# Stores on another queue, two weight splits earlier, one bank copy unpinned, and a reordered end of the down projection, in a one-core transformer layer

## The chip, the core and the metric

The kernel runs on one core of a Trainium2 chip. The metric is the device time of one execution in microseconds (us). A core has a matrix engine (TensorE, PE in the profile), a vector engine (DVE), a scalar engine (ACT), a general engine (POOL) and a queue that here only issues transfers (SP). Each engine takes its instructions in order; they wait for one another through semaphores. TensorE writes into PSUM, eight banks of 128 x 512 floats.

## The reference, cut to what matters

One layer on a sequence of 1024 tokens, width 1024, all float32:

```python
h = modulate(rms_norm(x, norm1_g), sh1, sc1)
q, k, v, g, hc, gb, gc = jnp.split(h @ w_in, 7, axis=-1)
# retention over q, k, v (4 heads, chunks of 64), a gated short convolution over hc, gb, gc
mixed = jnp.concatenate([ret_out, conv_out], axis=-1) @ w_out
x = x + gt1[:, None, :] * mixed
h = modulate(rms_norm(x, norm2_g), sh2, sc2)
u = causal_dwconv(h @ w_up, conv_ffn_w, conv_ffn_b)      # width 3, D_FF = 2816
ua, ub = jnp.split(u, 2, axis=-1)
x = x + gt2[:, None, :] * ((jax.nn.silu(ua) * ub) @ w_down)
return rms_norm(x, final_g)
```

## The kernel before

**Precision.** A float32 operand is split into a high half (a cast, mostly on ACT) and a low half (the difference, mostly on DVE), and each product is made of three matmuls: high x high, high x low, low x high. So nothing can be multiplied on PE before ACT and then DVE have worked on it.

**Tokens** are worked in 8 blocks (tb) of 128. The output projection runs in three groups, `out_mm((0, 1, 2))`, `out_mm((3, 4, 5))` and `out_mm((6, 7))`; in the last, block 7 lags a step behind block 6. Each step takes one of 8 pieces of w_out: a load into one of three raw buffers (SP, L923), the high half wo_h (ACT, L99), the low half wo_l (DVE, L100), each in one of four buffers.

**Per block**, `norm2` (L946 to L955) reloads x, multiplies the projection by the gate (DVE), adds it (L951; on DVE or POOL), stores the result as x1 (SP, L952), sums its squares (ACT, L165), makes the reciprocal root in two small POOL instructions (`rstd_of`, L159 and L160) and scales the row (DVE, L955). `norm2_T` transposes the scaled row on PE (x1T), modulates it on the way out of PSUM (ACT L989, DVE L991), and, for blocks 0 to 3, stores it as h_d (SP, L993) and splits it into h2[0]. For blocks 4 to 7 it reloads the row of block tb - 4 (hu) and forms the sums and differences that a seven-product (Strassen) scheme needs, splitting them into h2[1], h2[2] and h2[3].

**The up projection** works on 22 pairs of weight blocks (n), each in seven products over the banks X, Y and Z (`up_slots`). In front of the loop stand the products 1 and 2 of the first three pairs (N_EARLY), which need only h2[0] and the split weights a_h and a_l of the pair. `seed(n)` copies the sum of those products into bank Y (`Y<-p`); product 6 adds to it. The order inside the loop is written out by hand: `pin` (keep_in_program_order) holds instructions of an engine in the order of the program. What is not pinned is ordered by a scheduler when the program is built; it prefers what stands earlier in the program among what it thinks ready.

**The down projection** is seven products again, in the order 1, 6, 2, 5, 7, 4, 3, each over 11 operand pairs (`operands`: two loads into a ring, op_h on ACT L1266, op_l on DVE L1267, four buffers of each half). Between them partial sums are copied (f_, p7) and `gated_add` (two DVE instructions, L1326 and L1328) adds them to x1, which was loaded back. In the last product, blocks 4 to 7 are finished (`final`: squares, root, scale by final_g, store) and the left halves of blocks 0 to 3 are prepared (`left_half`); the last four operands are then taken block by block, and each block's right half is finished at once (`out_sum`, `out_scale`).

Of the kernel before, what the change touches and what calls it, by code (L numbers as in the profile page):

```python
# [11 lines left out]
F32 = mybir.dt.float32  # L12
# [3 lines left out]
ALU = mybir.AluOpType  # L16
# [54 lines left out]
def layer(ctx: ExitStack, tc: tile.TileContext, a: dict, out: bass.AP):  # L71
# [9 lines left out]
    def w4(name):  # L81
        return wk.tile([P, T], F32, tag="w4", name=name, bufs=6)
# [861 lines left out]
    def norm2(ps, tb, add):  # L944
        xt = w4(f"xr_{tb}")
        nc.sync.dma_start(xt, x[tb * P : (tb + 1) * P, :])  # L946
        t = w4(f"t1_{tb}")
        for ch in range(2):
            c = slice(ch * 512, (ch + 1) * 512)
            nc.vector.tensor_tensor(out=t[:, c], in0=ps[ch], in1=gt1[:, c], op=ALU.mult)  # L950
        add.tensor_tensor(out=xt, in0=t, in1=xt, op=ALU.add)  # L951
        nc.sync.dma_start(x1_d[tb], xt)  # L952
        ss = sumsq(xt, t, f"ss2_{tb}")
        r = rstd_of(ss, D, f"r2_{tb}")
        nc.vector.tensor_scalar(out=t, in0=xt, scalar1=r, scalar2=None, op0=ALU.mult)  # L955
        xn2[tb] = t
# [10 lines left out]
    def norm2_T(tb):  # L967
        t = xn2[tb]
        s = slice((tb % 4) * P, (tb % 4 + 1) * P)
        t3 = t.rearrange("p (k t) -> p k t", k=KT)  # L970
        if tb >= 4:
            u = w4(f"hu_{tb}")
            nc.sync.dma_start(u, h_d[tb - 4])
            u3 = u.rearrange("p (k t) -> p k t", k=KT)
        if tb < 6:
            pts = [r1k(f"x1T_{tb}_{q}") for q in range(2)]
        else:
            m = m2k(f"x1T_{tb}")
            pts = [m[:, h] for h in half]
        for q in range(2):  # L980
            for k in range(4):
                tr(pts[q][:, hs(k)], t[:, (4 * q + k) * P : (4 * q + k + 1) * P])
        for q in range(2):
            pt = pts[q]
            for i in range(4):
                k = 4 * q + i
                sc, sh = m2[:, k : k + 1], m2[:, 8 + k : 9 + k]
                if k % 2 or tb >= 4:
                    nc.scalar.activation(t[:, hs(k)], pt[:, hs(i)], AF.Identity, scale=sc, bias=sh)  # L989
                else:  # L990
                    nc.vector.tensor_scalar(out=t[:, hs(k)], in0=pt[:, hs(i)], scalar1=sc, scalar2=sh, op0=ALU.mult, op1=ALU.add)  # L991
        if tb < 4:
            nc.sync.dma_start(h_d[tb], t)  # L993
            split_h(h2[0], t3, s, KT)
            return
        tag = ("acc", "acc", "cos", "sin")[tb - 4]
        c = cst.tile([P, 512], F32, tag=tag, name=f"t3_{tb}", bufs=2 if tag == "acc" else 1)
        b12, b22, b11, b21 = t[:, half[0]], t[:, half[1]], u[:, half[0]], u[:, half[1]]
        tt(c, b22, b12, ALU.subtract)
        t3s[tb] = c  # L1000
        if tb >= 6:
            t3_split(tb)
        tt(b11, c, b11, ALU.add)
        tt(b21, b21, b11, ALU.subtract)
        split_h(h2[2], u3, s, KT)
        tt(b12, b22, b11, ALU.subtract)
        split_h(h2[1], t3, s, KT)
# [20 lines left out]
    h2[2] = slab.tile([P, 2, KT, 512], F32R, tag="S0", name="h2_2")  # L1028
    for tb in range(3, 6):
        norm2(ps[tb], tb, nc.vector if tb == 3 else nc.gpsimd)  # L1030
    ps = out_mm(
        (6, 7), "mm",
        {2: lambda _: norm2_T(3), 4: lambda _: norm2_T(4), 5: lambda _: norm2_T(5), 7: lambda ps: norm2(ps[6], 6, nc.vector)}, 1,
    )


    fseq = [j + i * NK for j in range(NK) for i in range(2)]
    NP = len(fseq)
# [6 lines left out]
    def A(o, i):  # L1045
        return pin(nc.scalar.copy(o, i))  # L1046
# [16 lines left out]
    def lo_of(n, key, put=V):  # L1063
        hi, lo, src, w = S[n][key]
        put(lo[:, :w], src, hi.bitcast(F32)[:, :w], ALU.subtract)

    for n in range(2):
        load_a(n)
        hi_of(n, "a", S[n]["wa"], nc.scalar.copy)
        lo_of(n, "a", tt)  # L1070
    norm2(ps[7], 7, nc.vector)
    mix_pool.__exit__(None, None, None)
    mlp_pool = tc.tile_pool(name="mlp_pool", bufs=1)
# [38 lines left out]

    def seed(n):
        y = S[n]["Y"] = bank_x(f"Y_{n}")
        if n == 0:

            mm(y, S[n]["a"][0][:, 0:P], h2[0][:, 0, 0])
        A(y, S[n]["p1"] if n < N_EARLY else S[n]["X"])

    def sum_a(n, V=V):  # L1120
        wa, wb = S[n]["wa"], S[n]["wb"]
# [56 lines left out]
    def up_slots(n):  # L1178

        old, new = n >= 1, n + 1 < NP  # L1180
        now = n < NP
        done = (n - 2) // 2 if n >= 2 and n % 2 == 0 else None
        early = n < N_EARLY
        if new:
            if n + 1 < N_EARLY or "wa" not in S[n + 1]:
                load_a(n + 1)
        if now:
            if not early:
                up_product(n, 1)
            lo_of(n, "b")  # L1190
        if old:
            A(S[n - 1]["ca"][:, half[1]], S[n - 1]["Y"])
            ident_(n - 1, "a")
        if now:
            sum_4(n)
            up_product(n, 7)
            lo_of(n, "4")
        if new:
            load_b(n + 1)
        if now:  # L1200
            seed(n)
        if old:
            ident_(n - 1, "b")
            tap(n - 1, "a", 1)
        if now:
            up_product(n, 6)
            S[n]["p7"] = mlp.tile([P, 512], F32, tag="p7", name=f"p7_{n}")
            A(S[n]["p7"], S[n]["Z"])
        if old:
            tap(n - 1, "a", 2)  # L1210
            tap(n - 1, "b", 1)
        if now:
            if not early:
                up_product(n, 2)
            S[n]["f"] = mlp.tile([P, 512], F32, tag="f", name=f"f_{n}")
            A(S[n]["f"], S[n]["Y"])
        if old:
            ta = S[n - 1]["ta"]
            pin(nc.scalar.activation(ta, ta, AF.Silu))  # L1219
            tap(n - 1, "b", 2)  # L1220
            V(ta, ta, S[n - 1]["tb"], ALU.mult)
        if now:
            up_product(n, 5)
            S[n]["ca"] = w4(f"ca_{n}")
            S[n]["cb"] = w4(f"cb_{n}")
        if new and n + 1 >= N_EARLY:
            hi_of(n + 1, "a", S[n + 1]["wa"])
            lo_of(n + 1, "a")
        if now:
            A(S[n]["ca"][:, half[0]], S[n]["X"])  # L1230
        if done is not None:
            acts_1(done)
        if now:
            up_product(n, 4)
            V(S[n]["cb"][:, half[1]], S[n]["Y"], S[n]["p7"], ALU.add)
        if done is not None:
            acts_2(done)
        if new:
            sum_a(n + 1)
        if now:  # L1240
            up_product(n, 3)
        if new:
            sum_b(n + 1)
        if now:
            V(S[n]["cb"][:, half[0]], S[n]["Z"], S[n]["f"], ALU.add)
        if new:
            lo_of(n + 1, "s")
# [35 lines left out]
    up_product(1, 2)  # L1283
    up_product(2, 1)
    first_out(2)
    norm2_T(7)
    up_product(2, 2)
    for n in range(NP):
# [52 lines left out]
    f_ = four("f")  # L1341
    for i in range(4):
        nc.scalar.copy(f_[i], pb[i])
    product(2, pa, False)
    for i in range(4):
        gated_add(i, 0, pa[i])
# [6 lines left out]
    for i in range(4):  # L1353
        nc.vector.tensor_tensor(out=p7[i], in0=pb[i], in1=p7[i], op=ALU.add)
        gated_add(4 + i, 1, p7[i])
    product(4, pa, False)
    for i in range(4):
        nc.vector.tensor_tensor(out=f_[i], in0=pa[i], in1=f_[i], op=ALU.add)
        gated_add(4 + i, 0, f_[i])
    pa = pb  # L1360

    def final(tb):
        y = w4(f"y_out_{tb}")
        ss = sumsq(x1[:, tb], y, f"ss3_{tb}")
        r = rstd_of(ss, D, f"r3_{tb}")
        nc.vector.scalar_tensor_tensor(out=y, in0=x1[:, tb], scalar=r, in1=fg, op0=ALU.mult, op1=ALU.mult)
        nc.sync.dma_start(out[tb * P : (tb + 1) * P, :], y)

    KB = NK - 4
    ys, s0 = {}, {}  # L1370

    def left_half(tb):

        ys[tb] = w4(f"y_out_{tb}")
        s0[tb] = square_half(tb, 0, ys[tb][:, half[0]], f"ss3_{tb}_0")
        pin(nc.gpsimd.tensor_scalar(out=s0[tb], in0=s0[tb], scalar1=1.0 / D, scalar2=EPS, op0=ALU.mult, op1=ALU.add))
        l = x1[:, tb, half[0]]
        pin(nc.vector.tensor_tensor(out=l, in0=l, in1=fg[:, half[0]], op=ALU.mult))

    ops3 = {j: operands(3, j) for j in range(4)}  # L1380
    for j in range(KB):
        for i in range(4):
            step_mm(pa, ops3[j], j, i, False)
        ops3[j + 4] = operands(3, j + 4)
        if 2 <= j < 6:
            final(j + 2)
        if 3 <= j < 7:
            left_half(j - 3)
    tail = ops3
    rs = {}  # L1390

    def out_sum(tb):
        t = f_[tb]
        pin(nc.vector.tensor_tensor(out=t, in0=pa[tb], in1=gt2[:, half[1]], op=ALU.mult))
        o = x1[:, tb, half[1]]
        pin(nc.vector.tensor_tensor(out=o, in0=t, in1=o, op=ALU.add))
# [78 lines left out]
```

## Time and profile before

| | us |
|---|---|
| median of three runs | 1169.44 (1167.85 to 1170.79) |
| the profiled execution | 1169.79 |
| its span, first to last instruction | 1167.9 |
| PE busy | 1115.9 (96%) |
| DVE busy | 821.6 (70%) |
| ACT busy | 504.9 (43%) |
| POOL busy | 120.4 (10%) |

The mean granted clock of PE is 0.983 of full speed. All 76,924 packets of the kernel's own transfers went through one queue, SP's (q1, 189.28 MB); POOL issued none. Matmuls are pipelined: the time listed for one is longer than the distance from one to the next.

### The profile page before, as it was taken

To read this page: it belongs to the slowest core of one execution; us is meant where nothing else is said; L and a number is where in the kernel's file an instruction comes from. 1 tells how busy PE (TensorE), PEld (TensorE's weight loads), DVE (VectorE), ACT (ScalarE), POOL (GpSimd) and SP (SyncE) were. 2 spreads that over 40 slices of the span, in tenths; PEclk is the share of its full clock that TensorE was granted. 3 is DMA by queue.
4 is the path that set the end of the run, shared out by engine and by line. 5 is a ranking of instruction groups with operands and counts; after the bars stand their busy time and mean duration, and the time that the engine had idled before them with its cause. 6 is when DMAs were issued, how large, how long until landed. Compare 5 with 4: busy or idle time off the path is not lost.

```text
span 1167.9 us, 13770 instructions
## 1 busy us (share of the span) xinstructions
PE 1115.9 (96%) x5093; PEld 920.8 (79%) x5093; DVE 821.6 (70%) x1107; ACT 504.9 (43%) x701; POOL 120.4 (10%) x143
## 2 busy tenths in 40 slices
PE   6999999999999899877999999999999999999995
PEld 5788888888887678655788888888888888888884
DVE  6956587676555477785988887888788874454676
ACT  6760122331111245654554554545455554433453
POOL 3503243100000111200000000000000000000034
PEclk9999999999999999888999999999999999999998
DMA  8732422267776456641323332323222389666543
GB/s 314 268 111 70 145 72 91 73 219 255 245 272 239 160 196 235 255 144 54 117 82 116 118 108 91 104 105 125 96 86 100 127 301 374 207 190 198 185 133 134
DMA packets 76991, 190.16 MB, mean 163 GB/s; under 512 B 8164, under 2 KB 8572, under 8 KB 76924
## 3 DMA queue, kind: packets, MB, share of 16 engines
q1 hardware_dynamic: 76924, 189.28, 47.2%
q8 instruction: 40, 0.66, 0.2%
q14 instruction: 27, 0.22, 0.1%
HBM read 146.52 MB, written 42.73 MB: 162 GB/s over the span
## 4 chain that ended last, share of the span: by engine, by line
PE 72%; DVE 10%; DMA 9%; ACT 4%; issue 3%; POOL 2%; SPq 0%; POOLq 0%; DVEq 0%; ACTq 0%
PE Y L113 15%; PE X L113 10%; PE Z L113 10%; PE pb L113 6%; PE pa L113 5%; PE pc L113 5%; PE po L113 5%; PE pq L113 4%; PE pk L113 4%; DMA wd<-in_w_down_dram 3%; PE pg L113 3%; PE pv L113 2%; DMA wo<-in_w_out_dram 1%; DMA wop<-wd 1%; DMA ada_g<-in_w_ada_dram 1%
## 5 line engine op out<-in xcount | busy, mean ns | idle before, releaser
L1267 DVE TENSOR_TENSOR op_l<-ring,op_h 128x1024 fp32r<-128x1024 f32 x74 | 89.8, 1223 | 78.9 <-ACT op_h L1266 74.4
L1266 ACT CAST op_h<-ring 128x1024 fp32r<-128x1024 f32 x74 | 78.0, 1054 | 104.6 <-PE pb L113 35.7
L113 PE MATMUL X<-h,a_h 128*128 128x512 f32 x352 | 110.1, 394 | 0.4 <-ACT p L1111 0.4
L113 PE MATMUL po<-wo_h,mix 128*128 128x512 f32 x256 | 85.0, 406 | 4.1 <-DVE y L872 3.6
L159 POOL TENSOR_SCALAR r<-ss 128x1 f32<-128x1 f32 x20 | 15.3, 767 | 661.3 <-ACT y_out L165 614.9
L113 PEld LDWEIGHTS X<-h,a_h 128*128 128x128 f32 x352 | 67.1, 191 | 14.6 <-ACT p L1111 0.6
L113 PE MATMUL X<-h,a_l 128*128 128x512 f32 x176 | 69.6, 396 | 7.5 <-DVE a_l L826 7.5
L1046 ACT CAST s_h<-st 128x1024 fp32r<-128x1024 f32 x21 | 22.1, 1054 | 102.0 <-DVE st L1043 102.0
L113 PEld LDWEIGHTS po<-wo_h,mix 128*128 128x128 f32 x256 | 49.9, 195 | 16.0 <-DVE y L872 4.0
L113 PE MATMUL Y<-h,s_h 128*128 128x512 f32 x176 | 56.3, 402 | 4.5 <-ACT Y L1046 4.5
L85 DVE SCALAR_TENSOR_TENSOR act<-ca,fcol,act 128x1023 f32<-128x1023 f32 (+1 forms) x44 | 56.3, 1281 | 1.3 <-ACT act L1143 0.5
L85 DVE SCALAR_TENSOR_TENSOR tb<-cb,fcol,tb 128x1023 f32<-128x1023 f32 (+1 forms) x44 | 56.3, 1280 | 0.7
L113 PE MATMUL Z<-h,s_h 128*128 128x512 f32 x176 | 54.6, 390 | 2.3 <-ACT h L964 2.1
L113 PE MATMUL Y<-h,b_h 128*128 128x512 f32 x176 | 54.5, 391 | 2.0 <-ACT f L1046 2.0
L113 PE MATMUL po<-wo_l,mix 128*128 128x512 f32 x128 | 51.7, 404 | 4.3 <-DVE wo_l L100 4.3
L113 PE MATMUL pb<-op_l,op_h 128*128 128x512 f32 x132 | 52.2, 396 | 3.3 <-DVE op_l L1267 3.3
L113 PE MATMUL Z<-h,b_h 128*128 128x512 f32 x176 | 54.2, 389 | 0.0
L113 PE MATMUL pb<-op_h,op_l 128*128 128x512 f32 x132 | 52.1, 395 | 0.0
L113 PE MATMUL pb<-op_h 128*128 128x512 f32 x132 | 52.0, 394 | 0.0
L113 PEld LDWEIGHTS X<-h,a_l 128*128 128x128 f32 x176 | 33.6, 191 | 15.0 <-DVE a_l L826 8.0
L99 ACT CAST wo_h<-wo 128x1024 fp32r<-128x1024 f32 x24 | 25.1, 1049 | 46.6 <-DMA wo<-in_w_out_dram 23.3
L1043 DVE TENSOR_TENSOR act<-act,tb 128x1024 f32<-128x1024 f32 x22 | 27.0, 1226 | 25.8 <-ACT act L1219 25.5
(438 smaller groups left out, 2990.2 us busy)
## 6 DMA issues: line engine op xcount, KB each, us to landing
ring<-aop SPq DMA_DIRECT2D x74, 256.0 KB
wa<-in_w_up_dram SPq DMA_DIRECT2D x25, 512.0 KB
wo<-in_w_out_dram SPq DMA_DIRECT2D x24, 512.0 KB
wd<-in_w_down_dram SPq DMA_DIRECT2D x22, 512.0 KB
wb<-in_w_up_dram SPq DMA_DIRECT2D x22, 512.0 KB
aop<-act SPq DMA_DIRECT2D x44, 256.0 KB
ring<-wop SPq DMA_DIRECT2D x44, 256.0 KB
aop<-s SPq DMA_DIRECT2D x33, 256.0 KB
```

Of the source, the lines that this page charges most:

```text
L85: return nc.vector.scalar_tensor_tensor(out=o, in0=i0, scalar=s, in1=i1, op0=ALU.mult, op1=ALU.add)
L99: c = nc.scalar.copy(hi, src)
L113: pin(nc.tensor.matmul(ps, st, mv, start=start, stop=stop, skip_group_check=more))
L159: q_(nc.gpsimd.tensor_scalar(out=r, in0=ss, scalar1=1.0 / n, scalar2=EPS, op0=ALU.mult, op1=ALU.add))
L1043: return pin(nc.vector.tensor_tensor(out=o, in0=i0, in1=i1, op=op))
L1046: return pin(nc.scalar.copy(o, i))
L1266: nc.scalar.copy(hi, raw)
L1267: nc.vector.tensor_tensor(out=lo, in0=raw, in1=hi.bitcast(F32), op=ALU.subtract)
```

## The change

It has five parts. The x1 stores and the h_d stores are issued by POOL instead of SP. The loads and splits of the first two pairs' up weights (`prep_a`) are written into the last output group: pair 0's after step 5, ahead of `norm2_T(5)`, pair 1's after step 6. `seed(0)` is called ahead of `norm2_T(7)` instead of inside `up_slots(0)`, and the seeds' copies of the first three pairs are not pinned any more. In the down projection, the left halves of blocks 4 to 7 get f_ added as soon as it is there, behind product 6, so that behind product 4 only pa is added. `left_half` of blocks 0 to 3 moves from the last product to behind product 7 and is not pinned; it has its own buffer for the squares. `final` is cut in two: squares and root (`final_a`) in steps 2 to 5, scale and store (`final_b`) one step later.

```diff
@@ norm2 @@
         add.tensor_tensor(out=xt, in0=t, in1=xt, op=ALU.add)
-        nc.sync.dma_start(x1_d[tb], xt)
+        nc.gpsimd.dma_start(x1_d[tb], xt)
@@ norm2_T @@
         if tb < 4:
-            nc.sync.dma_start(h_d[tb], t)
+            nc.gpsimd.dma_start(h_d[tb], t)
             split_h(h2[0], t3, s, KT)
@@ behind norm2 of blocks 3 to 5 @@
-    ps = out_mm(
-        (6, 7), "mm",
-        {2: lambda _: norm2_T(3), 4: lambda _: norm2_T(4), 5: lambda _: norm2_T(5), 7: lambda ps: norm2(ps[6], 6, nc.vector)}, 1,
-    )
...
-    for n in range(2):
+    def prep_a(n):
         load_a(n)
         hi_of(n, "a", S[n]["wa"], nc.scalar.copy)
         lo_of(n, "a", tt)
+
+    ps = out_mm(
+        (6, 7), "mm",
+        {2: lambda _: norm2_T(3), 4: lambda _: norm2_T(4), 5: lambda _: (prep_a(0), norm2_T(5)), 6: lambda _: prep_a(1), 7: lambda ps: norm2(ps[6], 6, nc.vector)}, 1,
+    )
     norm2(ps[7], 7, nc.vector)
@@ seed @@
         y = S[n]["Y"] = bank_x(f"Y_{n}")
+        put = nc.scalar.copy if n < N_EARLY else A
         if n == 0:
             mm(y, S[n]["a"][0][:, 0:P], h2[0][:, 0, 0])
-        A(y, S[n]["p1"] if n < N_EARLY else S[n]["X"])
+        put(y, S[n]["p1"] if n < N_EARLY else S[n]["X"])
@@ up_slots @@
         if now:
-            seed(n)
+            if n:
+                seed(n)
@@ in front of the loop over pairs @@
     first_out(2)
+    seed(0)
     norm2_T(7)
     up_product(2, 2)
@@ behind product 6 @@
         nc.scalar.copy(f_[i], pb[i])
+        gated_add(4 + i, 0, f_[i])
@@ behind product 7 @@
+    def left_half(tb):
+        s0[tb] = cst.tile([P, 1], F32, name=f"ss3_{tb}_0")
+        junk = w4(f"junk_{tb}")[:, half[0]]
+        nc.scalar.activation(junk, x1[:, tb, half[0]], AF.Square, accum_out=s0[tb])
+        nc.gpsimd.tensor_scalar(out=s0[tb], in0=s0[tb], scalar1=1.0 / D, scalar2=EPS, op0=ALU.mult, op1=ALU.add)
+        l = x1[:, tb, half[0]]
+        nc.vector.tensor_tensor(out=l, in0=l, in1=fg[:, half[0]], op=ALU.mult)
+
+    for tb in range(4):
+        left_half(tb)
     product(4, pa, False)
     for i in range(4):
-        nc.vector.tensor_tensor(out=f_[i], in0=pa[i], in1=f_[i], op=ALU.add)
-        gated_add(4 + i, 0, f_[i])
+        gated_add(4 + i, 0, pa[i])
@@ the last product @@
-    def final(tb):
+    def final_a(tb):
         y = w4(f"y_out_{tb}")
-        ss = sumsq(x1[:, tb], y, f"ss3_{tb}")
-        r = rstd_of(ss, D, f"r3_{tb}")
+        fin[tb] = y, rstd_of(sumsq(x1[:, tb], y, f"ss3_{tb}"), D, f"r3_{tb}")
+
+    def final_b(tb):
+        y, r = fin[tb]
         nc.vector.scalar_tensor_tensor(out=y, in0=x1[:, tb], scalar=r, in1=fg, op0=ALU.mult, op1=ALU.mult)
         nc.sync.dma_start(out[tb * P : (tb + 1) * P, :], y)
...
         if 2 <= j < 6:
-            final(j + 2)
-        if 3 <= j < 7:
-            left_half(j - 3)
+            final_a(j + 2)
+        if j >= 3:
+            final_b(j + 1)
```

## Rows read from the trace of the kernel before

**Rows 1.** Busy time by stretch of the span. Columns: the stretch and its length in us; then busy us (and instructions) of PE, PE's weight loads, DVE, ACT and POOL; the granted clock; the share of the transfer engines; GB/s.
```profile
467.00:482.00 15.00, 10.71 (x42) 8.47 (x41) 11.01 (x12) 5.52 (x9) 8.68 (x8) 0.77 0.54 206
498.60:511.60 13.00, 5.46 (x14) 4.03 (x13) 12.28 (x15) 4.74 (x8) 1.44 (x2) 0.61 0.35 118
530.00:545.00 15.00, 10.10 (x33) 7.51 (x33) 6.19 (x8) 4.70 (x7) 0.00 (x0) 0.77 0.22 70
560.00:944.00 384.00, 382.86 (x1687) 316.15 (x1686) 313.08 (x345) 197.19 (x243) 0.00 (x0) 1.00 0.32 108
944.00:1064.00 120.00, 120.00 (x531) 99.41 (x530) 66.57 (x61) 54.32 (x57) 0.00 (x0) 1.00 0.78 267
...
491.10:537.40 46.30, 32.05 (x138) 25.23 (x136) 37.16 (x46) 28.49 (x52) 2.18 (x4) 0.87 0.34 123
```

**Rows 2.** PE's instructions in order of time. Columns: start and duration in us, engine, line, operation, output<-inputs, shapes, count; in brackets the idle time before and what ended it.
```profile
475.96 0.79 PE L113 MATMUL po<-wo_l,mix 128*128 128x512 f32 x1 [4.29 <-DVE wo_l L100]
...
506.55 0.80 PE L113 MATMUL X<-h,a_l 128*128 128x512 f32 x1 [7.54 <-DVE a_l L826]
...
523.00 1.03 PE L121 MATMUL x1T<-small,t 128*128 128x128 f32 x8
...
529.53 0.50 PE L113 MATMUL Z<-h,s_h 128*128 128x512 f32 x1 [2.11 <-ACT h L964]
...
537.25 1.22 PE L113 MATMUL Y<-h,s_h 128*128 128x512 f32 x2 [4.00 <-ACT Y L1046]
```

**Rows 3.** The chain of work that ended last, in order of time. Columns: start and length in us, engine, name and line, number of instructions.
```profile
475.96 4.93 PE po L113 x11
...
506.55 10.24 PE X L113 x34
516.80 0.87 PE x1T L121 x8
...
537.25 5.25 PE Y L113 x12
...
542.52 0.59 ACT f L1046
...
543.16 3.02 PE Y L113 x12
...
1063.80 59.95 PE pc L113 x264
...
1148.71 10.55 PE pb L113 x38
```

**Rows 4.** DVE's and ACT's instructions around the first two early waits, in order of time; columns as in rows 2.
```profile
471.95 2.82 DVE L955 TENSOR_SCALAR t<-xr,r 128x1024 f32<-128x1024 f32 x1 [2.28 <-POOL r L160]
474.70 1.21 DVE L100 TENSOR_TENSOR wo_l<-wo,wo_h 128x1024 fp32r<-128x1024 f32 x1
...
478.49 2.35 DVE L100 TENSOR_TENSOR wo_l<-wo,wo_h 128x1024 fp32r<-128x1024 f32 x2
...
496.00 2.98 ACT L1061 CAST a_h<-wa 128x1024 fp32r<-128x1024 f32 x3
...
504.61 0.75 DVE L955 TENSOR_SCALAR t<-xr,r 128x1024 f32<-128x1024 f32 x1 [0.72 <-POOL r L160]
505.28 2.35 DVE L826 TENSOR_TENSOR a_l<-wa,a_h 128x1024 fp32r<-128x1024 f32 x2
...
514.76 0.75 DVE L955 TENSOR_SCALAR t<-xr,r 128x1024 f32<-128x1024 f32 x1
```

**Rows 5.** The same of DVE and ACT ahead of the third early wait.
```profile
535.33 0.68 DVE L1043 TENSOR_TENSOR wa<-wa,st 128x512 f32<-128x512 f32 x1
...
536.09 0.62 ACT L1046 CAST 4_0_h<-wa 128x512 fp32r<-128x512 f32 x1 [3.26 <-issue]
```

**Rows 6.** SP's issues, a POOL add and ACT's squares of one block around the first early wait; columns as in rows 2 (the SP row of three spans from the first issue to the end of the last).
```profile
467.90 6.67 SPq L952 DMA_DIRECT2D x_d<-xr  x3
476.00 0.33 SPq L923 DMA_DIRECT2D wo<-in_w_out_dram  x1
...
468.60 2.41 POOL L951 TENSOR_TENSOR xr<-t,xr 128x1024 f32<-128x1024 f32 x1 [26.30 <-DVE t L950]
...
468.37 1.05 ACT L165 ACTIVATE t<-xr 128x1024 f32<-128x1024 f32 x1
```

**Rows 7.** DVE, ACT and POOL in the last three products of the down projection, in order of time for each; columns as in rows 2.
```profile
1100.47 4.62 DVE L1267 TENSOR_TENSOR op_l<-ring,op_h 128x1024 fp32r<-128x1024 f32 x4
...
1123.29 1.28 DVE L1358 TENSOR_TENSOR f<-pc,f 128x512 f32<-128x512 f32 x2
...
1130.50 4.62 DVE L1267 TENSOR_TENSOR op_l<-ring,op_h 128x1024 fp32r<-128x1024 f32 x4
...
1147.44 1.22 DVE L1267 TENSOR_TENSOR op_l<-ring,op_h 128x1024 fp32r<-128x1024 f32 x1
...
1142.92 1.06 ACT L1266 CAST op_h<-ring 128x1024 fp32r<-128x1024 f32 x1 [1.41 <-issue]
...
1128.69 6.48 POOL L159 TENSOR_SCALAR r<-ss 128x1 f32<-128x1 f32 x1 [614.92 <-ACT y_out L165]
```

**Rows 8.** Waits from 1120 to the end. Columns: who waited, for whom, us in total, times, the longest in us.
```profile
PE pb L113 <- DVE op_l L1267: 3.3, 2, 2.5
DVE y_out L1366 <- POOL r L160: 2.0, 4, 0.7
```

More of the change, by code (lines that the diff above doesn't have):

```diff
@@ L1355, in layer @@
         gated_add(4 + i, 1, p7[i])
+    ys, s0 = {}, {}
+    def left_half(tb):
[7 more added lines that the diff above has]
+        left_half(tb)
     product(4, pa, False)
     for i in range(4):
-        nc.vector.tensor_tensor(out=f_[i], in0=pa[i], in1=f_[i], op=ALU.add)
-        gated_add(4 + i, 0, f_[i])
+        gated_add(4 + i, 0, pa[i])
     pa = pb
-    def final(tb):
+    fin = {}
+    def final_a(tb):
         y = w4(f"y_out_{tb}")
-        ss = sumsq(x1[:, tb], y, f"ss3_{tb}")
-        r = rstd_of(ss, D, f"r3_{tb}")
+        fin[tb] = y, rstd_of(sumsq(x1[:, tb], y, f"ss3_{tb}"), D, f"r3_{tb}")
+    def final_b(tb):
+        y, r = fin[tb]
         nc.vector.scalar_tensor_tensor(out=y, in0=x1[:, tb], scalar=r, in1=fg, op0=ALU.mult, op1=ALU.mult)
@@ L1369, in layer @@
     KB = NK - 4
[L1370 to L1378, printed above, removed]
     ops3 = {j: operands(3, j) for j in range(4)}
@@ L1393, in out_sum @@
         t = f_[tb]
+        ys[tb] = w4(f"y_out_{tb}")
         pin(nc.vector.tensor_tensor(out=t, in0=pa[tb], in1=gt2[:, half[1]], op=ALU.mult))
```

## The prediction

> **What bounds the kernel now.** I read the page first: PE is 96% busy and the chain of work that ended last is 72% PE, so only the time in which PE stands still, or runs slowly, can be won. Next the table of busy time by stretch [rows 1]. The steady part of the MLP (560 to 944: 382.86 of 384 us) and the first four products of the down projection (120.00 of 120.00) are full. There a matmul costs 384 / 1687 = 0.227 us. The losses sit in four other places; in the three early ones the granted clock is 0.61 to 0.77.
>
> Then PE's own order of time, where each wait shows what ended it [rows 2], the chain, whose rows show how long the matmuls behind a wait took [rows 3], and for the end the table of waits [rows 8]. Priced as the wait plus the slow matmuls behind it:
> - G1, at 471: 4.29 us for DVE's low half of an output weight, then 11 matmuls in 4.93 us instead of 11 x 0.227 = 2.50: 6.7 us.
> - G2, at 499: 7.54 us for DVE's low half of pair 0's up weight, then 34 in 10.24 instead of 7.72: 10.1 us.
> - G3, at 533: 4.00 us for ACT's copy into bank Y_0, then 12 in 5.25 instead of 2.72: 6.5 us.
> - G4, at 1144: two waits, 3.3 us, the longer 2.5, for DVE's low halves of the last operands, then 38 in 10.55 instead of 8.63: 5.2 us.
>
> After standing still for 4.29, 7.54 and 4.00 us PE works at about half pace for some matmuls: the lower of its two levels, 1.2 instead of 2.4 GHz. After the 2.11 us at 527 it does not. So closing a wait gives back its slow matmuls too. Then the order of time of the engine that PE waited for [rows 4, 5]: it was at other work, in order, or itself waiting.
>
> **Part 1: pair 0 and 1 split inside the last output group (G2).** ACT makes a_h of three pairs from 496.00, but DVE makes a_l only at 505.28, behind token block 5's transposition work and block 6's scale, which itself waits for POOL [rows 4]. With prep_a(0) written ahead of norm2_T(5), both halves stand in front of that work. PE then goes on at 498.6. Three up products (36 matmuls, 8.2 us), block 6's transposes (0.87) and two products (5.4) bring it to block 7's transposes at 513.1 instead of 523.0: 9.9 us at most. Late next is block 7's scaled row, which DVE finished at 514.76 + 0.75 = 515.5 [rows 4]; if it keeps that time, 7.5 us are won. If two a_l (1.22 each, 2.4) in front of it push it later, 5.1. DVE is the cover: it was busy 37.16 of the 46.3 us from 491.1 to 537.4 [rows 1], so the same list cannot end before 528.3, 9.1 earlier. I take 7.3, near the unchanged row, and keep 5.1 and 9.9.
>
> **Part 2: pair 0's copy, seed(0) before norm2_T(7), no longer pinned (G3).** The copy stood behind 4_0_h on ACT, and that behind DVE's wa at 535.33 [rows 5]. Its data, first_out of pair 0, were made right after the first product. Without it Y's product starts when Z ends, near 533.2, and takes 2.72. Late next is the copy f, which stays pinned behind 4_0_h and p: 536.09 with its 0.62, then p and f of 0.59 each (as f took), to 537.8 or a little less. The next product, at 543.16 before, starts near 537.8: 5.4 us. If DVE were quicker, it could be 6.6 (533.2 + 2.72 + 0.66, f's wait and copy as before). The same copies of pairs 1 and 2 lose their pin too; the steady part is full from 560, so nothing. I take 5.2.
>
> **Part 3: the stores on POOL's queue.** Twelve stores leave SP. SP issued each in about 0.33 us, and stood in front of them until the data came [rows 6]: behind the three x1 stores, 467.90 to 474.57, the next output weight load went at 476.00. That load gains nothing, as it needs the raw buffer that DVE's wo_l at 474.70 to 475.92 frees. POOL now issues them in order with its own adds and scales. No DMA issue on POOL is in this trace. From below it is 0.33, SP's row; the other end is 6.48, the longest row of a tiny POOL instruction, which ended with DVE's unbroken run at 1135.1 [rows 6, 7]. I take 1 us, between SP's 0.33 and POOL's 2.41 us adds, as DVE has breaks in those early stretches. For blocks 0 to 2 no PE wait follows in the trace, so the pieces behind have slack. In G1 none is left: block 3's scale waits for POOL's r until 471.92, and wo_l behind it; a store ahead of the add moves this by up to 1.2. I charge 1.2. The bounds are a gain of 2.1 (that scale took 2.82 us beside POOL's next add, and 0.75 at 504.61; a store could keep the add away) and a loss of 27 (under D). The h stores of blocks 0 to 2 fall into POOL's idle 26.30 us before 468.60; block 3's comes when its adds are done.
>
> What stands against this part: the longest POOL row shows POOL held by DVE, and the 2.82 us scale at 471.95 (0.75 at 504.61) is DVE held while POOL worked [rows 4, 7]. The Trainium skill's page "SBUF — State Buffer", section "SBUF: two separate sides", says that a DMA issued from POOL stalls while DVE holds the shared port pair, since its descriptors cannot be written, and advises SP or ACT instead. By it the stores would be stretched, as in rival D; no DMA in this trace can show it.
>
> **Part 4: the down end (G4).** DVE had 12 adds after product 4 (1123.29 to 1130.50), then four low halves back to back, then finals that waited for POOL, 2.0 us in four waits, and four multiplies by fg [rows 7, 8]. Out of this go four f adds (4 x 0.60 = 2.4), four multiplies (2.4) and the waits (2.0): 6.8 us. The last low half, done at 1147.44 + 1.22 = 1148.66, would be done by 1141.9, but its cast starts at 1142.92, when PE frees the buffer. With the cast's 1.06 and its own 1.22 it is done at 1145.2. PE, with nothing else late, would want it three operands (3 x 3 matmuls, 2.0) into the tail, at 1123.75 + 7 x 2.72 + 2.0 = 1144.8, so 0.5 to 0.8 us of waiting stays; with 0.8, 5.2 - 0.8 = 4.4 us (bounds 2 and 4.9).
>
> What moves elsewhere: eight gated adds (4.8 us) behind product 6. Eight like them stand behind product 2 already, and PE lost nothing from 944 to 1064 [rows 1], so nothing. The four squares and multiplies now stand behind product 7: there 12 adds end at 1100.47, the next low half at 1101.7, and product 4's fourth operand is due at 1063.80 + 11 x 2.72 + 3 x 2.72 = 1101.9 [rows 3, 7]. Margin 0.2: if the multiplies stand ahead of it, 2.4 - 0.2 = 2.2 us are lost. Their inputs are final since product 2, so they can run before, where DVE is busy 66.57 of 120.00 us; I take nothing and keep 2.2.
>
> **Sum.** 1169.79 (the profiled execution's own time; span 1167.9) - 7.3 - 5.2 - 4.4 + 1.2 = 1154.1. The median of the three runs is 0.35 below that execution, so 1154.
>
> **Rivals.**
> - A, as summed, 1149 to 1159: chance 0.55.
> - B, G1 closes as well, because DVE's order there is drawn up anew and wo_l goes ahead of the scales: 1154.1 - 1.2 - 6.7 = 1146. For it: wo_l itself waited for nothing at 474.70. Against: two more wo_l stand behind blocks 4 and 5 at 478.49, so the wait tends to move, not to go. 0.11.
> - C, a_l(0) is made no earlier than the norms, as DVE is 12.28 of 13.00 us busy there: part 1 gives nothing, 1154.1 + 7.3 = 1161.4; with the 2.2 of the multiplies 1163.6. 0.18.
> - E, the change does not do what it says: the two early parts give nothing, and only the down end is left: 1169.8 - 4.4 + 1.2 = 1166.6, within 0.3%. 0.08.
> - D, slower: POOL's stores take the place of the waits. Five stand on the path (blocks 3 to 5 in G1, 6 and 7 ahead of the transposes). Each may take 1.05 us unseen, the time of ACT's square beside it [rows 6]. At 6.48 each, 5 x 5.43 = 27 us: 1154.1 + 27 = 1181. It breaks even at 1.05 + 15.7 / 5 = 4.2 us a store. 0.08.
>
> **Numbers.** 0.3% (3.5 us) is about what a measurement of this kernel tells from no change. Faster by more: A, B and C, 0.84; within: E, 0.08; slower: D, 0.08. The range leaves out D, E and part of B and C: 1147 to 1163.5.
>
> **What would show it.** Part 1: a_l of pair 0 before 498 on DVE, and no PE wait at the first X matmul. Part 2: no wait for Y's copy, and f as the next. Part 3: POOL rows for 12 issues near 1 us, and G1 still there. Part 4: one wait under 1 us in product 3, and y_out on DVE without waits for POOL. It is wrong if block 7's transposes come after 518, if POOL's issues are over 4 us, or if PE waits at 1102.

## The result, and the profile after

The changed kernel takes 1159.05 us (median of four runs, 1154.24 to 1160.25) against 1170.12; the ratio is 0.9886 [0.9863, 0.9909]. Timed again later beside the kernel before, it took 1156.6 us against 1170.3, 0.988 [0.9859, 0.9902]. So it is faster by 1.1 to 1.2%, inside the range, and it won 11 to 14 us where the sum said 15.7. The profiled execution took 1159.58 us (span 1157.8), with a mean granted clock of 0.990.

First PE's order of time, as in [rows 2]; columns as there. Two rows of the kernel before come first, which give the start and the end of the stretch that the change touches: block 0's transposes and the last matmul.

```profile
448.15 1.04 PE L121 MATMUL x1T<-small,t 128*128 128x128 f32 x8
...
1158.86 0.39 PE L113 MATMUL pb<-op_h,op_l 128*128 128x512 f32 x1
```

The changed kernel:

```profile
450.76 1.03 PE L121 MATMUL x1T<-small,t 128*128 128x128 f32 x8
...
475.95 0.50 PE L113 MATMUL po<-wo_l,mix 128*128 128x512 f32 x1 [1.71 <-DVE wo_l L100]
...
479.30 1.09 PE L121 MATMUL x1T<-small,t 128*128 128x128 f32 x8 [0.56 <-DVE t L955]
...
500.29 0.73 PE L113 MATMUL X<-h,a_h 128*128 128x512 f32 x2 [0.32 <-ACT a_h L1056]
...
502.18 0.50 PE L113 MATMUL X<-h,a_l 128*128 128x512 f32 x1 [1.16 <-DVE a_l L826]
...
506.49 0.73 PE L113 MATMUL X<-h,a_h 128*128 128x512 f32 x2 [1.75 <-ACT p L1111]
...
512.42 1.09 PE L121 MATMUL x1T<-small,t 128*128 128x128 f32 x8 [2.90 <-DVE t L955]
...
520.67 1.03 PE L121 MATMUL x1T<-small,t 128*128 128x128 f32 x8
...
528.38 1.52 PE L113 MATMUL Z<-h,s_h 128*128 128x512 f32 x2 [3.95 <-ACT h L964]
...
537.70 0.73 PE L113 MATMUL Y<-h,b_h 128*128 128x512 f32 x2 [0.68 <-ACT f L1041]
...
1098.16 0.50 PE L113 MATMUL pc<-op_l,op_h 128*128 128x512 f32 x1 [1.93 <-DVE op_l L1269]
...
1149.97 0.39 PE L113 MATMUL pb<-op_h,op_l 128*128 128x512 f32 x1
```

Read the first row of each before anything else. Block 0's transposes stand ahead of all that the change could move but its first three stores, and yet they come 2.6 us later than in the profile of before. The stores are not the reason: from block 0's addition on DVE (L951), which is ahead of the first store, to these transposes it is 16.96 to 17.01 us in all fourteen profiles. Over these profiles the transposes lie between 447.28 and 451.19, whatever the kernel. Absolute times of two profiles therefore can't be compared here; I count from these transposes (T0). From T0 to the last matmul the kernel before took 710.7 us, the changed one 699.2: 11.5 us less.

G1's wait of 4.29 us became 1.71 and 0.56. G2's one wait of 7.54 became four of 0.32 to 2.90, the last in front of block 6's transposes. G3's wait for the Y copy is gone, and the copy f is next. But the longest wait that is left has grown: in front of the Z products, where PE waits for ACT's cast h, it is 3.95 us, 2.11 in [rows 2], and the matmuls behind it are slow (a granted clock of 0.69 from 528.38 to 537.70). A wait of 1.93 us is new, near 1098, in front of product 4's fourth operand. Busy time by stretch, columns as in [rows 1]:

```profile
467.00:482.00 15.00, 12.72 (x59) 9.96 (x59) 12.11 (x12) 6.42 (x10) 10.13 (x9) 1.00 0.59 208
498.60:511.60 13.00, 7.69 (x31) 5.06 (x29) 12.28 (x15) 7.74 (x12) 2.20 (x3) 1.00 0.57 195
530.00:545.00 15.00, 14.32 (x54) 11.28 (x54) 9.09 (x12) 6.60 (x10) 0.00 (x0) 0.86 0.21 70
560.00:936.00 376.00, 374.56 (x1652) 309.50 (x1651) 306.19 (x337) 194.19 (x239) 0.00 (x0) 1.00 0.32 108
936.00:1058.00 122.00, 122.00 (x540) 101.03 (x539) 72.49 (x71) 54.62 (x58) 0.00 (x0) 1.00 0.78 269
```

The granted clock at G1 and G2 is 1.00 (0.77 and 0.61 in [rows 1]). The steady part and the products up to 1058 are as full as before, with eight more additions on DVE. In the second row DVE is busy 12.28 of 13.00 us, the very number of before: PE gained, and DVE had little left to give in these 13 us. DVE's rows there, as in [rows 4]:

```profile
474.20 1.69 DVE L100 TENSOR_TENSOR wo_l<-wo,wo_h 128x1024 fp32r<-128x1024 f32 x1
476.35 2.89 DVE L955 TENSOR_SCALAR t<-xr,r 128x1024 f32<-128x1024 f32 x1 [0.46 <-POOL r L160]
...
493.70 0.69 DVE L826 TENSOR_TENSOR t<-t 128x512 f32<-128x512 f32 x1 [1.58 <-ACT t L989]
...
495.04 1.22 DVE L826 TENSOR_TENSOR a_l<-wa,a_h 128x1024 fp32r<-128x1024 f32 x1
...
500.91 1.22 DVE L826 TENSOR_TENSOR a_l<-wa,a_h 128x1024 fp32r<-128x1024 f32 x1
...
507.32 1.22 DVE L951 TENSOR_TENSOR xr<-t,xr 128x1024 f32<-128x1024 f32 x1
...
511.61 0.75 DVE L955 TENSOR_SCALAR t<-xr,r 128x1024 f32<-128x1024 f32 x1 [0.73 <-POOL r L160]
...
516.64 0.75 DVE L955 TENSOR_SCALAR t<-xr,r 128x1024 f32<-128x1024 f32 x1 [0.73 <-POOL r L160]
```

wo_l now stands ahead of the scale; in [rows 4] it stood behind it. Pair 0's a_l comes at 495.04 instead of 505.28, and block 6's scaled row at 511.61 instead of 504.61. Some of POOL's issues and one of its additions in its order of time, columns as in [rows 2]:

```profile
435.33 0.77 POOL L952 DMA_DIRECT2D x_d<-xr  x1 [26.08 <-DVE xr L951]
...
470.73 0.53 POOL L952 DMA_DIRECT2D x_d<-xr  x1 [4.80 <-DVE xr L951]
...
476.30 2.39 POOL L951 TENSOR_TENSOR xr<-t,xr 128x1024 f32<-128x1024 f32 x1
478.64 0.73 POOL L952 DMA_DIRECT2D x_d<-xr  x1
...
480.48 0.58 POOL L952 DMA_DIRECT2D x_d<-xr  x1
...
488.09 0.60 POOL L993 DMA_DIRECT2D h_d<-t  x1 [4.13 <-ACT t L989]
```

### The profile page after: what moved, and what is told of

It reads as the page before. It is cut to its first block, busy times and chain, and to the rows that moved or that the text cites. A ratio compares the mean times of both kernels' runs of the same rounds, so it can differ in the third digit from the quotient of the medians.

```text
span 1157.8 us, 13789 instructions
## 1 busy us (share of the span) xinstructions
PE 1112.6 (96%) x5093; PEld 918.5 (79%) x5093; DVE 827.7 (71%) x1111; ACT 505.2 (44%) x701; POOL 120.8 (10%) x155
## 4 chain that ended last, share of the span: by engine, by line
PE 67%; DVE 14%; DMA 10%; ACT 4%; issue 3%; POOL 1%; SPq 0%; POOLq 0%; DVEq 0%; ACTq 0%
PE Y L113 14%; PE Z L113 10%; PE X L113 10%; PE pb L113 8%; PE pa L113 5%; PE pc L113 4%; PE pk L113 4%; DMA wd<-in_w_down_dram 4%; PE po L113 3%; PE pq L113 3%; PE pg L113 2%; PE pv L113 2%; DMA wo<-in_w_out_dram 2%; DVE tc L826 1%; DMA ada_g<-in_w_ada_dram 1%
## 5 line engine op out<-in xcount | busy, mean ns | idle before, releaser
L100 DVE TENSOR_TENSOR wo_l<-wo,wo_h 128x1024 fp32r<-128x1024 f32 x24 | 31.4, 1316 | 17.1 <-ACT wo_h L99 17.1
```

The lines of the kernel that those rows point to most:

```text
L100: d = nc.vector.tensor_tensor(out=lo, in0=src, in1=hi.bitcast(F32), op=ALU.subtract)
```

## The experiments

All times are medians. The six columns in the middle come from each run's profile: the start of block 0's transposes (T0), and from there the us to block 3's, 6's and 7's transposes, to pair 0's product `Y<-h,b_h` (537.70 above) and to the start of the last matmul. The last column is the ratio to the kernel before, timed beside it. e7 leaves out two stores, so its outputs are other numbers.

| kernel | T0 | block 3 | block 6 | block 7 | pair 0 | last | us | ratio |
|---|---|---|---|---|---|---|---|---|
| before | 448.15 | 32.6 | 68.5 | 74.9 | 95.0 | 710.7 | 1170 to 1172 | |
| changed | 450.76 | 28.5 | 61.7 | 69.9 | 86.9 | 699.2 | 1159.05 | 0.9886 |
| e11, changed again | 447.28 | 28.5 | 61.5 | 69.8 | 86.4 | 698.6 | 1156.60 | 0.9880 |
| e1, stores alone | 450.24 | 28.6 | 67.3 | 73.6 | 94.9 | 710.5 | 1170.16 | 0.9990 |
| e2, split alone | 451.19 | 32.7 | 61.8 | 69.8 | 90.6 | 706.3 | 1166.49 | 0.9962 |
| e5, seed alone | 449.15 | 31.8 | 67.7 | 74.2 | 89.6 | 705.6 | 1166.95 | 0.9960 |
| e6, down end alone | 448.51 | 32.9 | 68.8 | 75.1 | 94.5 | 707.2 | 1167.28 | 0.9974 |
| e3, changed, stores on SP | 449.11 | 32.6 | 61.7 | 70.0 | 87.0 | 699.3 | 1158.30 | 0.9896 |
| e4, changed, X first | 451.19 | 28.5 | 61.3 | 66.1 | 84.2 | 698.1 | 1157.49 | 0.9887 |
| e7, changed, two stores out | 449.70 | 28.5 | 61.3 | 67.9 | 84.4 | 696.7 | 1156.13 | 0.9872 |
| e8, changed, left halves early | 449.89 | 28.5 | 61.5 | 69.8 | 86.4 | 696.5 | 1154.16 | 0.9856 |
| e9, X first and left halves | 450.73 | 28.5 | 61.4 | 66.1 | 84.4 | 694.5 | 1153.88 | 0.9852 |
| e12, the same again | 449.56 | 28.5 | 61.6 | 66.3 | 84.6 | 694.6 | 1152.89 | 0.9847 |
| e10, and block 5 later | 449.12 | 28.5 | 58.7 | 63.0 | 84.1 | 694.1 | 1154.77 | 0.9849 |

### Part 3 alone, and the change without it (e1, e3)

e1 on the kernel before; e3 is the reverse of it on the changed kernel.

```diff
-        nc.sync.dma_start(x1_d[tb], xt)
+        nc.gpsimd.dma_start(x1_d[tb], xt)
-            nc.sync.dma_start(h_d[tb], t)
+            nc.gpsimd.dma_start(h_d[tb], t)
```

> The kernel before with part 3 alone: the twelve x1 and token stores issued by POOL instead of SyncE. Theory T1 (the stores cost POOL about 0.6 us each, and what they really do is move the multiplication's place: VectorE splits wo ahead of scaling block 0 of the second group, and takes pair 0's a_l further up its queue): the first gap near 471 closes from 4.3 us to under 2 us with the granted clock at 1.00, about 4 us less; 1164 to 1167 us. Rival T2 (the stores delay POOL's root and so the scaled row, as the prediction had it): the gap at 471 grows by 1 to 2 us; 1171 us. Rival T3 (the stores change nothing and G1 closed because of the split): 1170 us, gap 4.3 us.

> The changed kernel with the twelve stores back on SyncE. T1: the first gap is back at 4 us, the rest as in the changed kernel: 1162 to 1164 us. Rival T2 (the stores on POOL load the DMA engines earlier, wo's last load takes 7.6 us and delays everything to 500): the first gap is back, but 2.5 us are won behind it: 1160 to 1161 us. Rival T3 (the queue does not matter): 1159 us.

Ratios: e1 0.999 [0.9977, 1.0002], e3 0.9896 [0.9877, 0.9916]. PE's order of time in e1:

```profile
475.48 0.50 PE L113 MATMUL po<-wo_l,mix 128*128 128x512 f32 x1 [1.72 <-DVE wo_l L100]
...
511.08 0.79 PE L113 MATMUL X<-h,a_l 128*128 128x512 f32 x1 [9.05 <-DVE a_l L826]
```

The stores alone close G1, as T1 said: block 3's transposes come 4.0 us sooner. But G2's wait grows from 7.54 to 9.05 with another 1.77 ahead of it, and at pair 0 only 0.2 us are left. In e3, G1 is back (4.49 us), and by block 6 nothing of it is seen. PE's order of time in e3:

```profile
477.08 0.79 PE L113 MATMUL po<-wo_l,mix 128*128 128x512 f32 x1 [4.49 <-DVE wo_l L100]
```

So T1's total was wrong, and T3's "the queue does not matter" is right for the time, by two effects that cancel: the first gap is back and as much is won back behind it, which is T2's account with 4 us where it had 2.5. What takes the 4 us back stands in the chain of the changed kernel (columns as in [rows 3]):

```profile
482.09 7.64 DMA wo<-in_w_out_dram
...
489.81 1.05 ACT wo_h L99
490.86 1.35 ACT t L989 x4
```

In the chain of e3 PE itself set the pace:

```profile
482.74 5.50 PE po L113 x24
488.23 0.02 issue
488.25 1.05 ACT wo_h L99
489.30 1.41 ACT t L989 x4
```

ACT takes its work in order, so the evacuation of block 4's transposes waits behind the cast of the last output weight. With the stores on POOL, PE is 4 us ahead, and the cast waits for the load (7.64 us) instead. DVE begins to split block 4 at 43.0 us after T0 in the kernel before and in e3, at 42.9 in the changed one (the row at 493.70).

### Part 1 alone (e2)

```diff
-        {2: ..., 4: ..., 5: lambda _: norm2_T(5), 7: ...}, 1,
+        {2: ..., 4: ..., 5: lambda _: (prep_a(0), norm2_T(5)), 6: lambda _: prep_a(1), 7: ...}, 1,
```

> The kernel before with part 1 alone: pair 0's and pair 1's weights prepared inside the last output group. T1 (VectorE works through its queue without a gap from 495 to 520, so what is taken up early pushes block 6's sum and scaled row back): PE's 7.4 us wait at 499 falls to small waits, but a new one of 2 to 4 us stands at block 6's transposes, and the transposes of block 7 come only 1 to 3 us earlier against the kernel before; 1167 to 1169 us. Rival P (the prediction's term): 7.3 us less, 1163 us, transposes of block 7 at 513 to 518. Rival T2 (with the stores on SyncE the weights for the last step of the output group land 2.5 us earlier than in the changed kernel, and that was what ate the gain): 1165 to 1166 us, a wo wait of ScalarE near 0 at 487.

0.9962 [0.9947, 0.9977]; 4.4 us by the profile, between T1's figures and the prediction's. The place was as T1 said, but T1's 1 to 3 us at block 7's transposes are 5.1. T2's sign is there too (ACT does not wait for a load of wo), and its 1165 to 1166 us is nearer than T1's time; but without that wait e2 still stands still in front of block 6's transposes, so that load is not what took part 1's gain. PE's order of time in e2:

```profile
513.01 1.26 PE L121 MATMUL x1T<-small,t 128*128 128x128 f32 x8 [3.11 <-DVE t L955]
...
528.83 1.52 PE L113 MATMUL Z<-h,s_h 128*128 128x512 f32 x2 [3.94 <-ACT h L964]
...
536.55 0.72 PE L113 MATMUL Y<-h,s_h 128*128 128x512 f32 x2 [1.81 <-ACT Y L1040]
```

The last two rows matter for the sum: with part 1 alone the wait for the Z products has grown from 2.11 to 3.94 us, and the wait for the Y copy, 4.00 us in [rows 2], is already down to 1.81.

### Part 2 alone (e5), part 4 alone (e6)

e5, with `seed(0)` taken out of `up_slots` as in the change:

```diff
+        put = nc.scalar.copy if n < N_EARLY else A
-        A(y, S[n]["p1"] if n < N_EARLY else S[n]["X"])
+        put(y, S[n]["p1"] if n < N_EARLY else S[n]["X"])
...
     first_out(2)
+    seed(0)
     norm2_T(7)
```

e6 has the change's diff from "behind product 6" to its end, and nothing else of it.

> The kernel before with part 2 alone: pair 0's bank copy unpinned and called ahead of block 7's transposes. Theory U (the parts add: 5 us from part 1, 3 to 4 from part 2, nothing from part 3, 3 from part 4, counted from block 0's transposes on, since everything ahead of them differs by up to 3 us between executions): 1167 to 1168 us against 1171; the 4.0 us wait of the Y copy gone, the Y products that follow it by 3 to 4 us earlier. The prediction's term: 5.2 us, 1166 us. Rival H (hidden: block 7's normalized rows end last whatever the copy does): under 1 us, 1170 to 1171 us.

> The kernel before with part 4 alone, the down end. Theory U: 5.1 us won in product 3 and 2.2 lost in front of product 4's fourth operand, 2.9 net: 1168 us against 1171, with a PE wait of about 2 us near 1102. The prediction's term: 4.4 us and no wait there: 1166.8 us. Rival H: the two cancel, 1171 us.

e5: 0.996 [0.9941, 0.9979], the Y copy's wait gone, 5.1 us by the profile: near the prediction's 5.2, more than theory U gave it. e6: 0.9974 [0.9958, 0.9989], 3.5 us, with a wait of 1.92 us for op_l at 1103.94. The four parts alone come to 0.2 + 4.4 + 5.1 + 3.5 = 13.2 us, the change to 11.5. Not all of the 1.7 between them is overlap: 0.6 of e5's gain already stands at block 7's transposes and 0.6 of e6's at pair 0, ahead of what their edits touch, so a single figure here is good to about half a microsecond. From block 7's transposes to pair 0, e5 gains 4.8; behind part 1, part 2 brings 3.7, so the two share about 1.

### The left halves (e8)

`product` gets a list of calls: behind step j + 4 of product 5 stands the left half of block j.

```diff
             for i in range(4):
                 step_mm(ps, op, j, i, start)
+            if lh and j in lh:
+                left_half(lh[j])
...
-    product(5, pb, False)
+    product(5, pb, False, {j + 4: j for j in range(4)})
...
-    for tb in range(4):
-        left_half(tb)
     product(4, pa, False)
```

> The changed kernel with the left halves of blocks 0 to 3 (their squares and four multiplications) called inside product 5, one behind each of the steps 4 to 7, instead of ahead of product 4. Theory U (those four multiplications, 2.5 us of VectorE, are the 1.9 us wait for product 4's operand): the wait near 1098 is gone, 2.0 to 2.2 us less from product 7's start to product 3's, 1157 us where the changed kernel has 1159. Rival F (the eight additions ahead of them keep the operand late): 1 us wait left, 1158 us.

0.9856 [0.9832, 0.9879]; 1154.16 us. No PE wait is listed from 1060 to 1160, and from pair 0 to the last matmul PE takes 610.0 us instead of 612.3. In the changed kernel DVE's order of time had them ahead of the operand:

```profile
1094.48 2.49 DVE L1369 TENSOR_TENSOR x<-x,fg 128x512 f32<-128x512 f32 x4
1096.89 4.62 DVE L1269 TENSOR_TENSOR op_l<-ring,op_h 128x1024 fp32r<-128x1024 f32 x4
```

### What is left of the early stretch (e4, e7, e9, e10)

e4, and in e9 and e10 too:

```diff
-    norm2_T(6)
     up_product(1, 2)
+    norm2_T(6)
```

e7, with x in the place of x1 where blocks 4 and 5 are loaded back:

```diff
-        nc.gpsimd.dma_start(x1_d[tb], xt)
+        if tb not in (4, 5): nc.gpsimd.dma_start(x1_d[tb], xt)
```

e9 is e4 and e8 together; e10 is e9 with

```diff
-        5: lambda _: (prep_a(0), norm2_T(5)), ..., 7: lambda ps: norm2(ps[6], 6, nc.vector)
+        5: lambda _: prep_a(0), ..., 7: lambda ps: (norm2(ps[6], 6, nc.vector), norm2_T(5))
```

> The changed kernel with pair 1's second X product called ahead of block 6's transposes, so that TensorE has 2.7 us of work in the 2.9 us wait in front of them. T1 (that wait and the low clock behind it, 4.4 us together, are what is left of the gain of part 1): transposes of block 7 from 520.7 to 516.5 to 517.5 us, and 1 to 3 us of it kept at the Z products, whose wait is for block 7's normalized rows on ScalarE: 1156 to 1158 us. Rival D (VectorE and ScalarE bound the stretch up to 530 us whatever TensorE's order): the Z wait grows by what the transposes win; 1159 us.

> The changed kernel without the x1 stores of blocks 4 and 5 (the down phase adds onto x there, so their outputs are other numbers). Theory C (collision: on POOL's queue these two 512 KB stores start at 478 and 480, beside wo's last load of 7.6 us, and that is what takes back the 4 us that TensorE wins at the first gap): the load takes 4 to 5 us, ScalarE's 1.0 us wait for it is gone, block 6's transposes stand 59 to 60 us behind those of block 0 instead of 61.7: 1156 to 1158 us. Rival V (VectorE's queue from block 4's splitting to block 6's scaling sets it): 61.5 us, 1159 us.

> The changed kernel with both edits, X product of pair 1 ahead of block 6's transposes and the left halves inside product 5. Theory U (the two stand in different stretches and add): pair 0's fifth product 84.2 us behind block 0's transposes as in the run with the first edit alone (86.9 in the changed kernel), no wait near 1095, 1152 us, a ratio of 0.983 to 0.985 to the kernel before. Rival: one of them is hidden, 1154 to 1155 us.

> As the run with both edits, and block 5's transposes and splitting called behind block 6's norm, so that VectorE comes to block 6's sum and scaled row some 4 to 5 us earlier; nothing is left out. Theory V (VectorE's queue, block 6's row behind the splitting of block 5, is what took back the rest of part 1's gain): block 6's scaled row 4 us earlier, no wait for block 6 or 7's transposes, the Z products 1 to 3 us earlier: 1149 to 1151 us. Rival W (the work of VectorE and ScalarE up to the Z products is the same in any order and sets them): the transposes earlier, the wait for the Z products longer by as much, 1152 us.

In e4 block 7's transposes come 3.8 us sooner after T0, and pair 0 2.7: T1's figure, though 1.6 of it are lost again in product 4 (last section), and the time alone (1157.49) could not have told. In e7 the chain's last load of wo reads

```profile
483.14 5.17 DMA wo<-in_w_out_dram
```

so with the two stores out that load takes 5.17 us, not 7.64. But block 6's transposes stand at 61.3, not 59 to 60 as theory C had it. The run does not settle C, though: the load is also issued 2 us later from T0, its raw buffer coming free only then, so what the shorter load alone would give is not shown. Of the 2.5 us that e7 has at pair 0, 1.6 are won between block 6's and block 7's transposes and 0.9 from the first Z product to pair 0 (8.39 us, 9.32 in the changed kernel), in both places at a higher granted clock (last section).

e9 took 1153.88 us, between U's 1152 and its rival's 1154 to 1155; in the profile the two edits add as U said, pair 0 at 84.4 as in e4 (84.2) and 610.1 us from there to the last matmul as in e8 (610.0).

e10 puts theory V to the test. The wait in front of block 6's transposes is gone, and block 7's come 3.1 us before e9's. But the wait went on to the next place, which is not the Z products that W had named; PE's order of time in e10:

```profile
517.47 1.22 PE L113 MATMUL X<-h,a_h 128*128 128x512 f32 x2 [4.27 <-ACT p L1111]
...
524.68 0.50 PE L113 MATMUL Z<-h,s_h 128*128 128x512 f32 x1 [2.14 <-ACT h L964]
```

Pair 0 gains 0.4, the time nothing (0.9849 against 0.9852): W's figure. Busy time from the first split of block 4 to the first Z product, columns as in [rows 1]. The kernel before:

```profile
491.10:530.00 38.90, 28.88 (x125) 22.91 (x123) 31.00 (x39) 25.19 (x47) 2.18 (x4) 0.87 0.39 140
```

The changed kernel:

```profile
493.70:528.40 34.70, 24.62 (x106) 18.84 (x104) 30.47 (x39) 25.51 (x47) 4.18 (x6) 0.94 0.41 144
```

e10:

```profile
492.00:524.70 32.70, 25.03 (x111) 19.42 (x109) 30.27 (x39) 25.66 (x48) 3.71 (x6) 0.90 0.47 158
```

The third busy number of each row is DVE's: it has the same 39 instructions, 30.3 to 31.0 us, in all three. Its idle time is 7.9, 4.2 and 2.4 us. As long as these 39 stand ahead of the first Z product, that idle time is the most that another order of PE's work could win here; how much of the last 2.4 can be had no run shows.

### The two again, on one chip (e11, e12)

> The changed kernel itself, on the chip of the next run. Theory U (the four parts add up to 11 to 12 us, and what differs between its runs is the stretch ahead of 450 us and the clock in two gaps): 1157 to 1160 us, ratio 0.9886 within 0.002; first to last matmul of the changed stretch (block 0's transposes to the last matmul) 699 us in the profile. Rival (the first four runs were lucky or unlucky): under 1156 or over 1161 us.

> The version with both edits beside the changed kernel on one chip. Theory U: 4.7 us below the changed kernel (694.5 against 699.2 us from block 0's transposes to the last matmul), 1153 to 1155 us. Rival: no more than the 2.2 us of the left halves, 1157 us.

The changed kernel 1156.6 us, 0.988 [0.9859, 0.9902], a little under U's band; the version with both edits 1152.89, 0.9847 [0.9824, 0.987]. The 3.7 us between them are 4.0 in the profiles. That version beats both kernels, by about 17 us and 4 us. e9 and e12 differ in nothing but the run.

## Why the prediction was right, and where it was not

The direction, the places and the range held. Of its own three alarms one went off clearly, PE's wait in front of product 4's fourth operand. Block 7's transposes came at 520.7, after 518; counted from T0 that is 518.1 on the clock of the profile before, just at the mark. By its terms:

**Part 1, 7.3 predicted, 4.4 measured (e2), below the lower bound of 5.1.** What was predicted of the weights came true: a_l at 495.04 on DVE, before 498, and G2's 7.54 us gone. The step that failed is "late next is block 7's scaled row". It was block 6's, one block earlier. Two a_l and the two last low halves of block 5 went ahead of its sum, and its scale moved from 504.61 to 511.61, 4.4 us of that beyond the later start of the run. At block 7's transposes e2 does win 5.1 us (74.9 to 69.8), the lower bound's very number, but by luck: PE does not wait for block 7's row there, it comes late from block 6's. And what is won there was not kept: the wait in front of the Z products, which the prediction left as it was, grew from 2.11 to 3.94 us. The prediction had the right kind of bound in the same paragraph, DVE's own list, and used it only as a check. Taken from block 4's split to the Z products, it leaves 7.9 us of idle DVE, of which the changed kernel used about half; e10, which used more, brought pair 0 only 0.4 us beyond e9.

**Part 2, 5.2 predicted, 5.1 alone (e5; 4.8 from block 7's transposes to pair 0), 3.7 behind part 1** (90.6 to 86.9 at pair 0). The mechanism and the next in line, f at 537.06 behind 4_0_h and p, came as written. What failed is the addition: part 1 had already shortened the Y wait to 1.81 us (e2), since both waits end on the same lists of DVE and ACT.

**Part 3, 1.2 lost predicted, 0.2 won (e1), 0.1 (e3 against the changed kernel).** An issue on POOL takes 0.53 to 0.77 us in the 12 rows, not 1. G1 was predicted to stay, and closed: rival B's mechanism, wo_l ahead of the scales, by the stores alone. The scale itself did come later, as was feared, from 23.8 to 25.6 us after T0; but wo_l no longer stood behind it (26.6 to 23.4). B's price of 6.7 failed, for the wait moved on, as the text against B said, though to another place than it named: to the load of wo and ACT's cast.

The Trainium skill's page "SBUF — State Buffer", section "SBUF: two separate sides", was cited for rival D: a DMA issued from POOL stalls while DVE runs an operation that holds the port pair which the two share. Here none of the 12 issues took more than 0.77 us, though DVE was at work beside eight of them, at least in part; so D's stretching did not come about. Whether DVE held the pair at those times no row tells, so the rule itself is not tested.

**Part 4, 4.4 predicted, 3.4 measured.** From pair 0 to the last matmul PE took 615.7 us before, 612.3 after and 610.0 in e8. So G4 gave 5.7, somewhat over the 5.2 at which the wait was priced, and the left halves cost 2.2, the very sum that the text worked out, took as nothing and kept for the range. "They can run before" was true of the data and not of the order in which the instructions were laid: unpinned, they still stood behind the twelve additions. The eight additions behind product 6 cost nothing, as predicted.

The misses add up: 2.9 in part 1, 1.5 in part 2 and 1.0 in part 4, less the 1.2 charged for part 3, which behind the others cost nothing (e3): the 4.2 us between 15.7 and 11.5. That the total came out nearer than its terms is luck to that extent, a loss charged that did not come.

What stays open: why DVE's and ACT's lists come out as they do is known only from their order, the bound by DVE's idle time is argued from its busy time and not forced by a run, and a version that closes the last 2.4 us of DVE's idle time was not tried.

## What to carry to other kernels

Ahead of pricing several waits one by one, add up what the engine behind them has to do in the whole stretch: as long as that work has to be done ahead of the stretch's end, the engine's idle time is the most that they can give together, and waits with one engine behind them share it. Of a moved split, name the first thing that falls behind it in the queue, not the one that PE needs last. And count from an event that the change can't touch: here the start of the stretch moved by up to 3.9 us between runs, as much as a part was worth.

## What the runs showed of the hardware

The same wait keeps the clock in one run and loses it in another. In front of block 6's transposes PE waited 2.90 us in the changed kernel and in e7. In the changed kernel it ended at 512.42, and the stretch behind it is this, columns as in [rows 1]:

```profile
512.40:518.00 5.60, 5.58 (x22) 4.60 (x23) 4.87 (x8) 3.42 (x7) 1.98 (x3) 0.70 0.48 181
```

In e7 it ended earlier; its row in PE's order of time, and the two stretches that hold what came behind it:

```profile
510.99 1.09 PE L121 MATMUL x1T<-small,t 128*128 128x128 f32 x8 [2.90 <-DVE t L955]
```

```profile
506.00:512.40 6.40, 3.50 (x21) 2.71 (x20) 5.67 (x7) 1.43 (x3) 2.19 (x3) 1.00 0.94 298
512.40:518.00 5.60, 5.60 (x28) 4.63 (x27) 4.57 (x8) 5.60 (x13) 1.70 (x3) 1.00 0.30 123
```

The granted clock is 0.70 in the changed kernel, a part of the stretch at 1.2 GHz, and 1.00 in both of e7's. What differs ahead of it: the changed kernel had also stood still for 0.32, 1.16 and 1.75 us, e7 for 0.30 and 1.71. From block 6's transposes to block 7's it took 8.25 and 6.63 us: 1.6 us for the clock. Likewise product 4's wait, 1.93 us in the changed kernel and 1.94 in e4. The changed kernel's stretch with that wait, which ended at 1098.16:

```profile
1090.00:1104.00 14.00, 12.07 (x54) 9.66 (x53) 12.73 (x17) 6.81 (x13) 1.71 (x4) 1.00 0.27 94
```

e4's, where it ended at 1095.90:

```profile
1090.00:1104.00 14.00, 12.06 (x47) 9.47 (x46) 10.48 (x13) 5.79 (x11) 1.75 (x4) 0.88 0.48 152
```

e4 lost 1.6 us more there. So the price of a wait of 2 to 3 us was, in these runs, the wait and in some of them 1.6 us behind it. Why one profile lost the clock and another did not stays open.

A scale on DVE of 0.75 us took 2.89 us beside a POOL addition (476.35 and POOL's row at 476.30 above), as the 2.82 of [rows 4], while POOL's issues stayed under 0.8 us: in these profiles it was the addition, not the issue of transfers, that came with a stretched scale.
